# Six modulation vectors by one-column and broadcast matmuls, an opening without a stop, and a dense layer's last block by token tile

## Chip, cores and metric

One core of one Trainium2 chip runs the whole network. The metric is the device time of one execution in microseconds (us). The engines are TensorE (PE, matmuls), VectorE (DVE), ScalarE (ACT), GpSimd (POOL) and SyncE (SP, which issues the loads of weights).

## What is computed

Eight residual steps act on 256 tokens of width 1024. Each is conditioned on a vector c: a step's shift, scale and gate are slices of silu(c) @ w + b, and its input is h = norm(x) * (1 + scale) + shift. The layer inside a step is a mixer (steps 1 and 3), a dense SwiGLU of inner width 2816 (steps 2, 6 and 8), eight routed experts (step 4) or two kinds of attention (steps 5 and 7).

```python
def modulation(c, w, b):
    m = jnp.einsum("bd,de->be", jax.nn.silu(c), w) + b
    shift, scale, gate = jnp.split(m, 3, axis=-1)

def swiglu(h, w1, w3, w2):
    a = jnp.einsum("btd,df->btf", h, w1)
    g = jnp.einsum("btd,df->btf", h, w3)
    return jnp.einsum("btf,fd->btd", jax.nn.silu(a) * g, w2)

# steps 1 to 4 (layers 0 and 1): post-norm with a gain and a bias
x = layer_norm(DN_ALPHA * x + (1.0 + gate) * y, post_ln_g[layer, i], post_ln_b[layer, i])
# steps 5 to 8: h from rms_norm(x), and
x = x + g_a * (o @ w_out[l])
```

## The kernel before

The two token tiles of 128 (t = 0, 1) stay on chip throughout, and every weight is read once, in loads of 1 MB (`raw`, four buffers). A dense product is made of three passes (lines 178 to 180): ACT rounds the weight into a high part (line 159), DVE makes the low part by subtraction (line 160), and PE multiplies high by high, low by high and high by low. All engines run their own queues in order; a scheduler fixes the order of each queue when the program is built, from priorities. `behind()` keeps work that is issued early behind a step's residual, and `self.free` counts the weight splits that may pass this bar; before, that is the first split after step 1.

A modulation vector (layer, part, name) is written (l, s, SC), (l, s, SH) or (l, s, GA) for scale, shift and gate. Its 1024 x 1024 slice of w comes in four loads. `plan` says in which step a vector is made, for use one step later (a gate: at the end of the step after its scale's use begins); `fill(n)` spreads the loads over the step. There are two ways:

- `mod_rows` (line 301): DVE multiplies each row block of w by the entry of silu(c) that belongs to its partition and adds up, eight operations of 128 x 1024 (lines 318 and 320), into `macc`. `mod_done` then sums over partitions on PE: for a scale or shift eight matmuls with `macc` as the stationary operand and a column of ones (line 348), for a gate two matmuls of 512 columns with a matrix of ones.
- `mod_gate_pe` (line 281), for the gate (0, 0) alone: 16 matmuls of 512 columns multiply the raw weight by a broadcast entry of silu(c), in fp32, plus one per half for the bias row.

The opening (`run`): `setup` makes small constants; x is loaded and normalized; `fill(KD * KD)` makes (0,0,SC) and then (0,0,SH) by `mod_rows`, the column of the one being finished on PE and DVE ahead of the other's first product; then the rest of `setup` (`columns`, line 402: three transposes and copies) and `make_h` (line 511), which transposes x, applies scale and shift and splits the result for the projections.

The routing at step 4: `fill(KD * KD)` makes (2,0,SC), (2,0,SH) and (2,0,GA), all used in step 5, then `make_hf` transposes x, and `route` multiplies by the router, picks two experts a token and builds the lists that `experts` works through. `resid_rms` (line 591) ends the step with the gate (1,1).

A dense layer (`ffn`, line 673) runs over 11 blocks of 256 inner columns: project both halves, silu, multiply, and two blocks later `down` adds the block's part of the output to four accumulators (two token tiles by two halves). The last two blocks' `down` runs at the end, for t = 0 and then for t = 1:

```python
        for t in range(2):
            self.down(accs, [b for q in pend for b in block(*q)], t)
```

`resid` (line 549) follows, tile by tile: multiply by the gate (line 558), add x, statistics, and the normalized tile (line 586 or 588).

Of the kernel before, what the change touches and what calls it, by code (L numbers as in the profile page):

```python
# [19 lines left out]
D = 1024  # L20
# [47 lines left out]
class _Net:  # L68
# [82 lines left out]
    def split_now(self, v):  # L151

        k, n = v.shape[1], v.shape[2]
        H, L = [], []
        for z in range(0, k, k // 2):
            m = k // 2
            h = self.tl("hi", [128, 1024], F32R)[:, :m * n].rearrange("p (k n) -> p k n", k=m)
            l = self.tl("lo", [128, 1024], F32R)[:, :m * n].rearrange("p (k n) -> p k n", k=m)
# [23 lines left out]
    def mm(self, out, lhsT, rhs, start=True, stop=True):  # L182
        self.nc.tensor.matmul(out, lhsT=lhsT, rhs=rhs, start=start, stop=stop)  # L183
# [116 lines left out]
    def mod_rows(self, key):  # L300
# [13 lines left out]
        for i in range(2):  # L314
            k = self.modpos + i
            c = self.csil[:, c0 + k:c0 + k + 1]
            if k == 0 and not row:
                V.tensor_scalar(acc, v[:, i], c, None, ALU.mult)
            else:
                V.scalar_tensor_tensor(acc, v[:, i], c, acc, ALU.mult, ALU.add)  # L320

    def mod_done(self, key):

        if key in self.gates_pe:
# [11 lines left out]
        c = self.tl("col", [128, KD])  # L336
# [9 lines left out]
        else:  # L346
# [3 lines left out]
            sums = p[:, 0:KD]  # L350
        q = ((l * 2 + s) * 3 + j) * KD if l < 2 else ((l - 2) * 6 + j) * KD
# [4 lines left out]
    def mod(self, l, s, name):  # L356
        assert (l, s, name) in self.mods, (l, s, name)
        return self.mods[(l, s, name)]


    def setup(self):
# [19 lines left out]
        nc.gpsimd.memset(self.zero, 0.0)  # L381
        p = self.ps()
# [3 lines left out]
        self.off = {}  # L386

        def stack(tag, names, eng):

            r = self.sc([128, 128])  # L390
# [10 lines left out]
        def columns(tag, r, q):  # L401
            p = self.ps()
# [22 lines left out]
        self.identb = self.tl("const", [128, 128], BF16, tag="identb")
        V.tensor_copy(self.identb, self.ident)
        self.maskb = self.tl("const", [128, 384], BF16, tag="maskb")
        nc.gpsimd.memset(self.maskb, 0.0)
        V.tensor_copy(self.maskb[:, 0:128], cst[:, C_NEG:C_RT])
        V.tensor_copy(self.maskb[:, 256:384], cst[:, C_NEG:C_RT])  # L430
# [118 lines left out]
    def resid(self, get, x, gate, ln, norm=True):  # L549
# [39 lines left out]
        if norm:  # L589
            self.bar, self.free = self.last.ins, self.step == 1  # L590
# [85 lines left out]
    def ffn(self, h, w1, w3, w2, fill):  # L676
# [10 lines left out]
        for i in range(nstep):  # L687
            pss = []
            if i == 0:
# [15 lines left out]
            W2 = self.wrow(w2, 2 * i)  # L705
# [795 lines left out]
    def run(self):  # L1501
        a, nc = self.a, self.nc
        FFN = dict(f=2, s2=10, sh=12, pp=4, pa=4)
# [9 lines left out]
            0: [(0, 0, SC), (0, 0, SH)],  # L1513
# [3 lines left out]
            4: [(2, 0, SC), (2, 0, SH), (2, 0, GA)],  # L1517
# [4 lines left out]
        self.gates_pe = {(0, 0, GA)}  # L1522
# [3 lines left out]
        with self.phase(sh=12, s1=1, s2=3, pp=4, pa=4):  # L1526
            setup = self.setup()
            next(setup)
            self.mod_start(plan[0])
            x = self.load_x(a["x"])  # L1530
            xn = x = self.layer_norm(x)
            self.fill(KD * KD)
            for _ in setup:
                pass
            g, b = self.c1("ln0_g", 0), self.c1("ln0_b", 0)
            self.later = [lambda x=x: self.affine(x, a["ln0_g"], a["ln0_b"])]
        for s in range(1, 9):
# [5 lines left out]
            with self.phase(**SIZES[s]):  # L1543
# [4 lines left out]
                if s == 4:  # L1548
# [67 lines left out]
```

## Time and profile before

| what | value |
|---|---|
| device time, median of 3 runs | 2068.33 us (2067.39 to 2068.36) |
| the profiled execution: its own time / span of its trace | 2068.1 / 2066.0 us |
| busy: PE / DVE / ACT / POOL | 1926.2 / 1643.8 / 1208.2 / 50.2 us |
| bytes moved; mean rate | 555.25 MB; 269 GB/s |
| stretches: head, steps 1, 2, 3 | 0 to 45, to 175, to 377, to 513 us |
| routing, experts, step 5 | 513 to 564, to 1365, to 1524 us |
| steps 6, 7, 8 with the store | to 1726, to 1862, to 2066 us |

A stretch ends where PE's last matmul of the step does. Times in the trace count from the span's start. A matmul's duration includes its way through the array, so neighbours overlap, and what one costs is the distance between starts. A matmul in fp32 shows as two records, or, where the trace joins equal neighbours, as a row with their count (x16). The square bracket at a row's end is the time its engine was idle just before and the instruction that ended the wait. "PEclk" is the mean clock that TensorE was granted, as a share of 2.4 GHz; it has two levels, 1.00 and 0.50. Up to 50 us the profile shows 1.00 because nothing is recorded before the first change; there durations tell.

### The profile page before, as it was taken

Reading aid. Unit: us, or ns where it says so; the run is one execution under the profiler, and the core shown is the slowest. Engines: PE = TensorE matmul, PEld = TensorE weight load, DVE = VectorE, ACT = ScalarE, POOL = GpSimd, SP = SyncE. Lnnn points to the kernel's source line nnn. Section 1 sums busy time; section 2 is a strip of 40 time slices with the busy share of each in tenths; the row PEclk is TensorE's granted clock in tenths of the full one; section 3 lists DMA queues with packets and bytes.
Section 4 is the critical chain, followed back from the end, with each engine's and each line's share of the span. In section 5 each row is a group of like instructions: output and inputs, shape, how many; then the busy total and the mean of one; then the engine's idle time right before and its main releaser. Section 6 shows DMA issues by size and latency. Waiting matters only on the chain.

```text
span 2066.0 us, 29939 instructions
## 1 busy us (share of the span) xinstructions
PE 1926.2 (93%) x11481; PEld 1660.4 (80%) x11481; DVE 1643.8 (80%) x2412; ACT 1208.2 (58%) x1817; POOL 50.2 (2%) x100
## 2 busy tenths in 40 slices
PE   3998999898499999999999999969989999998999
PEld 3887999886378787878778888858869998978998
DVE  6888987898598888888888888889778887667554
ACT  3455445562488767767776777755554546555442
POOL 4000000100000000000000000000000000000000
PEclk9999999998699999999999999979999999999999
DMA  9576999665399999899999999958339995326662
GB/s 325 184 276 214 348 329 316 195 223 205 144 330 362 339 332 341 319 357 346 345 326 350 348 355 358 364 187 279 138 119 349 335 328 164 123 86 220 204 204 82
DMA packets 283238, 555.25 MB, mean 269 GB/s; under 512 B 10172, under 2 KB 137520, under 8 KB 283088
## 3 DMA queue, kind: packets, MB, share of 16 engines
q1 hardware_dynamic: 280000, 549.49, 75.1%
q0 software_dynamic: 2656, 3.20, 0.9%
q8 instruction: 91, 1.49, 0.3%
q10 hardware_dynamic: 432, 0.58, 0.1%
q14 instruction: 59, 0.48, 0.1%
HBM read 552.19 MB, written 1.05 MB: 268 GB/s over the span
## 4 chain that ended last, share of the span: by engine, by line
PE 63%; DVE 6%; ACT 2%; issue 2%; DMA 0%; ACTq 0%; DVEq 0%
PE pp L179 11%; PE pp L180 11%; PE pp L178 11%; PE pa L654 6%; PE ya L179 4%; PE ya L178 4%; PE ya L180 4%; PE pp L187 3%; DVE lo L160 2%; PE pj L178 2%; PE pj L179 1%; PE pj L180 1%; PE sa L183 1%; PE pp L183 1%; ACT hi L159 1%
## 5 line engine op out<-in xcount | busy, mean ns | idle before, releaser
L160 DVE TENSOR_TENSOR lo<-raw,hi 128x1024 fp32r<-128x1024 f32 x660 | 786.0, 1219 | 177.3 <-ACT hi L159 168.6
L159 ACT CAST hi<-raw 128x1024 fp32r<-128x1024 f32 x660 | 667.4, 1050 | 344.2 <-PE pp L179 141.8
L178 PE MATMUL pp<-h,hi 128*128 128x256 f32 x960 | 270.7, 282 | 0.0
L180 PE MATMUL pp<-h,lo 128*128 128x256 f32 x960 | 267.8, 279 | 0.0
L179 PE MATMUL pp<-h,hi 128*128 128x256 f32 x960 | 267.7, 279 | 0.0
L160 DVE TENSOR_TENSOR lo<-rawx,hi 128x1024 fp32r<-128x1024 f32 x176 | 208.3, 1219 | 40.2 <-ACT hi L159 38.9
L320 DVE SCALAR_TENSOR_TENSOR macc<-raw,const,macc 128x1024 f32<-128x1024 f32 x168 | 215.2, 1281 | 9.9 <-DMA raw<-in_w_mod_dram 7.1
L180 PEld LDWEIGHTS pp<-h,lo 128*128 128x128 f32 x960 | 182.2, 190 | 0.1
L159 ACT CAST hi<-rawx 128x1024 fp32r<-128x1024 f32 x176 | 176.9, 1050 | 9.2 <-PE pp L180 7.4
L179 PEld LDWEIGHTS pp<-h,hi 128*128 128x128 f32 x960 | 180.6, 188 | 1.7 <-issue 1.2
L178 PEld LDWEIGHTS pp<-h,hi 128*128 128x128 f32 x960 | 180.3, 188 | 1.7 <-ACT hi L159 1.0
L179 PE MATMUL pp<-lo,h 128*128 128x512 f32 (+1 forms) x480 | 174.9, 365 | 1.3 <-DVE lo L160 1.0
L178 PE MATMUL pj<-hi,h 128*128 128x256 f32 x576 | 168.3, 293 | 7.2 <-ACT h L530 4.0
L178 PE MATMUL pp<-hi,h 128*128 128x512 f32 (+1 forms) x480 | 173.5, 362 | 0.2 <-ACT f L528 0.2
L179 PE MATMUL pj<-lo,h 128*128 128x256 f32 x576 | 165.1, 288 | 1.8 <-DVE lo L160 1.8
L180 PE MATMUL pj<-hi,h 128*128 128x256 f32 x576 | 164.8, 288 | 0.0
L654 PE MATMUL pa<-hi,s 128*128 128x512 f32 x528 | 148.2, 390 | 0.0
L179 PE MATMUL pp<-lo,xe 128*128 128x512 f32 (+1 forms) x384 | 144.9, 377 | 1.2 <-DVE lo L160 1.0
L180 PE MATMUL pp<-hi,x 128*128 128x512 f32 (+1 forms) x384 | 143.7, 374 | 0.0
L178 PE MATMUL pp<-hi,xe 128*128 128x512 f32 (+1 forms) x384 | 143.6, 374 | 0.0
L180 PE MATMUL pp<-hi,xe 128*128 128x512 f32 (+1 forms) x384 | 143.1, 373 | 0.0
L179 PE MATMUL ya<-lo,s 128*128 128x512 f32 x352 | 140.8, 400 | 0.0
(474 smaller groups left out, 3518.5 us busy)
## 6 DMA issues: line engine op xcount, KB each, us to landing
raw<-in_moe_w_dram SPq DMA_DIRECT2D x176, 1024.0 KB, 6.3
rawx<-in_moe_w_dram SPq DMA_DIRECT2D x88, 1024.0 KB, 6.3
raw<-in_ada_w_dram SPq DMA_DIRECT2D x48, 1024.0 KB, 6.7
raw<-in_w_mod_dram SPq DMA_DIRECT2D x48, 1024.0 KB, 6.9
raw<-in_w_in_dram SPq DMA_DIRECT2D x42, 1024.0 KB, 6.0
raw<-in_ffn_w_dram SPq DMA_DIRECT2D x33, 1024.0 KB, 6.3
raw<-in_w_gate_dram SPq DMA_DIRECT2D x22, 1024.0 KB, 5.2
raw<-in_w_up_dram SPq DMA_DIRECT2D x22, 1024.0 KB, 5.3
```

Of the source, the lines that this page charges most:

```text
L159: self.nc.scalar.copy(h, v[:, z:z + m])
L160: self.nc.vector.tensor_tensor(l, v[:, z:z + m], h.bitcast(F32), ALU.subtract)
L178: mm(out, lhsT=a[0], rhs=b[0], start=start, stop=False)
L179: mm(out, lhsT=a[0], rhs=b[1], start=False, stop=False)
L180: mm(out, lhsT=a[1], rhs=b[0], start=False, stop=stop)
L183: self.nc.tensor.matmul(out, lhsT=lhsT, rhs=rhs, start=start, stop=stop)
L187: self.nc.tensor.transpose(out, in_, self.ident[:p, :p])
L320: V.scalar_tensor_tensor(acc, v[:, i], c, acc, ALU.mult, ALU.add)
L654: mm(accs[t][h], lhsT=y[ia][:, s], rhs=W[ib][:, h * 512:(h + 1) * 512], start=start and ia == 0 and ib == 0, stop=stop and ia == 1)
```

## The change

Five things change. (1) `mod_first` opens the program: the shift's first product goes to ACT, DVE runs through both vectors' products, the columns are finished after both, and 20 bf16 matmuls of zeros (`warm`) stand on PE between the scale's and the shift's column matmuls; `setup` yields twice more, so that one of its copies is made early and two after `make_h`. (2) `mod_cols_pe` makes (0,1,SH), (2,0,SC), (2,0,SH) and (2,1,SH): per load 16 matmuls of one column with the raw weight as the stationary operand and an entry of silu(c) as the moving one, and a small DVE addition. (3) The gates (1,1) and (2,0) go through `mod_gate_pe`; (2,0,GA) moves from the routing to behind the experts. (4) `ffn` works its last block by token tile, in the natural layout (tokens on partitions), with four transposes more, and W2 of the block before has pools of its own (`wh`, `wl`). (5) Two splits may pass the bar after steps 2 and 6.

```diff
@@ def fill
                 if key in self.gates_pe:
                     self.mod_gate_pe(key)
+                elif key in self.cols_pe:
+                    self.mod_cols_pe(key)
@@
+    def mod_cols_pe(self, key):
...
+        v = self.raw(wv[:, self.modpos:self.modpos + 2, j * D:(j + 1) * D])
+        p = self.ps(pool=self.mps)
+        for q in range(KD):
+            for i in range(2):
+                k = c0 + self.modpos + i
+                self.mm(p[:, q:q + 1], v[:, i, q * 128:(q + 1) * 128], self.csil[:, k:k + 1], i == 0, i == 1)
+        if self.modpos == 0:
+            V.scalar_tensor_tensor(self.modacc, p[:, 0:KD], 1.0 if key[2] == "scale" else 0.0, self.mod_bias(key), ALU.add, ALU.add)
+        else:
+            V.tensor_tensor(self.modacc, self.modacc, p[:, 0:KD], ALU.add)
@@ def mod_rows
-            if k == 0 and not row:
+            if k == 0 and act:
+                nc.scalar.activation(acc, v[:, i], ACT.Copy, scale=c)
+            elif k == 0 and not row:
@@
+    def warm(self, p, n, after):
+
+        with self.tc.issue_after(after):
+            for _ in range(n):
+                self.nc.tensor.matmul(p.rearrange("p (q n) -> p q n", n=128), lhsT=self.zero[:, 0:128], rhs=self.zero[:, None, :].to_broadcast([128, 4, 128]), start=True, stop=True)
+
+    def mod_first(self, scale, shift, setup):
+
+        V = self.nc.vector
+        ps = []
+        for key in (scale, shift):
+            for k in range(0, KD, 2):
+                self.modpos = k
+                self.mod_rows(key, key == shift)
+            p = self.ps()
+            for k in range(KD):
+                self.mm(p[:, k:k + 1], self.modacc[:, k * 128:(k + 1) * 128], self.ones[:, 0:1])
+            ps.append(p)
+            if key == scale:
+                next(setup)
+                self.warm(self.ps(), 20, self.pe_last.ins)
+        with self.tc.issue_after(self.mod_last.ins):
+            next(setup)
+            for key, p in zip((scale, shift), ps):
+                self.mods[key] = self.mod_col(key, p[:, 0:KD])
@@ def resid
-            self.bar, self.free = self.last.ins, self.step == 1
+            self.bar, self.free = self.last.ins, {1: 1, 2: 2, 6: 2}.get(self.step, 0)
@@ def ffn
-        for t in range(2):
-            self.down(accs, [b for q in pend for b in block(*q)], t)
+
+        Ws = [self.wcol(w, i * 256) for w in (w1, w3)]
...
+        for t in range(2):
+            s = slice(t * 128, (t + 1) * 128)
+            for p, W in zip(pss, Ws):
+                for k in range(KD):
+                    self.mm3(p[:, t], (h[0][:, k, s], h[1][:, k, s]), (W[0][k], W[1][k]), k == 0, k == KD - 1)
+            S.activation(sa[:, t], pss[0][:, t], ACT.Silu)
+            V.tensor_tensor(gn[:, t], sa[:, t], pss[1][:, t], ALU.mult)
+            for q in pend:
+                self.down(accs, block(*q), t)
+            for j in range(2):
+                self.tr(gp[:, j, s], gn[:, t, j * 128:(j + 1) * 128])
...
+            self.down(accs, block((gh, gl), W2, i), t)
@@ def run
-            4: [(2, 0, SC), (2, 0, SH), (2, 0, GA)],
+            4: [(2, 0, SC), (2, 0, SH)],
...
-        self.gates_pe = {(0, 0, GA)}
+        self.gates_pe = {(0, 0, GA), (1, 1, GA), (2, 0, GA)}
+        self.gps = "pa"
+        self.cols_pe = {(0, 1, SH), (2, 0, SC), (2, 0, SH), (2, 1, SH)}
...
-            self.fill(KD * KD)
-            for _ in setup:
-                pass
+            self.mod_first((0, 0, SC), (0, 0, SH), setup)
...
                     get = lambda t, hh: ysum[t][hh]
+
+                    self.gps = "pp"
+                    self.mod_start([(2, 0, GA)])
+                    self.fill(KD)
+                    self.gps = "pa"
```

PE's queue before, at step 4's routing, from the last matmul of step 3 to the router's matmuls (`macc` 5419 and 5447 are the scale and the shift (2,0), 5475 is the gate (2,0), `x` the normalized tokens, `sh` the router):

```order
L654 MATMUL pa_5189<-hi_5274,h_4720 128x512
L183 MATMUL pp_5437<-const_115,macc_5419 128x1 x8
L183 MATMUL pp_5465<-const_115,macc_5447 128x1 x8
...
L183 MATMUL pp_5495<-macc_5475,const_115 128x512
L183 MATMUL pp_5498<-macc_5475,const_115 128x512
L187 MATMUL pp_5502<-const_113,x_5327 128x128 x4
...
L187 MATMUL pp_5523<-const_113,x_5327 128x128 x4
L183 MATMUL pp_5532<-sh_5530,h_5501 128x8 x16
```

Here the transposes stand behind 16 column matmuls and the gate's two.

The same place of PE's queue now (`raw` are loads of the scale and the shift (2,0), `const_127` is silu(c)):

```order
L719 MATMUL pa_5283<-hi_5368,h_4814 128x512
L182 MATMUL pp_5516<-const_127,raw_5514 128x1 x16
L182 MATMUL pp_5536<-const_127,raw_5534 128x1 x16
...
L182 MATMUL pp_5637<-const_127,raw_5635 128x1 x16
L182 MATMUL pp_5657<-const_127,raw_5655 128x1
L186 MATMUL pp_5676<-const_113,x_5421 128x128 x4
L182 MATMUL pp_5657<-const_127,raw_5655 128x1 x15
...
L186 MATMUL pp_5697<-const_113,x_5421 128x128 x4
L182 MATMUL pp_5706<-sh_5704,h_5675 128x8 x16
```

There are now 128 column matmuls in eight groups, seven groups and one matmul of them ahead of the first transpose, and the gate is gone.

PE's queue now in step 1, toward the end of the mixer (`raw` are loads of the shift (0,1), `pj` is a projection, L715 begins the output projection):

```order
L177 MATMUL pj_1516<-hi_1512,h_348 128x256
L182 MATMUL pa_1420<-const_127,raw_1418 128x1
L178 MATMUL pj_1516<-lo_1513,h_348 128x256
L182 MATMUL pa_1420<-const_127,raw_1418 128x1
L179 MATMUL pj_1516<-hi_1512,h_349 128x256
L182 MATMUL pa_1420<-const_127,raw_1418 128x1 x5
L182 MATMUL pa_1577<-const_127,raw_1575 128x1 x16
L182 MATMUL pa_1597<-const_127,raw_1595 128x1 x16
L715 MATMUL pj_1653<-raw_1657,ml_1101 128x512
```

Two of the four groups alternate with a projection's matmuls, and two stand back to back; before, DVE did this sum and eight column matmuls followed.

PE's queue now behind the experts (`ya` is their sum, `pa` the residual's input, `raw` 16898 to 16919 the gate (2,0)'s loads, `x` the normalized tokens of step 5):

```order
L179 MATMUL ya_16036<-hi_16859,s_16828 128x512
L182 MATMUL pp_16896<-raw_16898,const_127 128x512
L182 MATMUL pa_5754<-s_16875,s_14869 128x512
...
L182 MATMUL pp_16896<-raw_16898,const_127 128x512 x3
L182 MATMUL pp_16896<-raw_16904,const_127 128x512 x4
L182 MATMUL pp_16911<-gate_16894,const_115 128x512
L182 MATMUL pp_16911<-raw_16913,const_127 128x512 x4
L182 MATMUL pp_16911<-raw_16919,const_127 128x512 x4
...
L186 MATMUL pp_17035<-const_113,x_16930 128x128 x4
```

The gate's 16 matmuls came in between the residual's input and the transposes for step 5; on SP's queue its four loads stand ahead of `post_ln_g`, `post_ln_b` and step 5's first weights.

## Rows read from the trace of the kernel before

**Rows 1.** The page: busy us (share of the span) and instructions of each engine.

```profile
PE 1926.2 (93%) x11481; PEld 1660.4 (80%) x11481; DVE 1643.8 (80%) x2412; ACT 1208.2 (58%) x1817; POOL 50.2 (2%) x100
```

**Rows 2.** Busy time by stretch (start:end, length, busy us of PE, PEld, DVE, ACT, POOL, PEclk, DMA).

```profile
50.00:175.00 125.00, 124.56 (x792) 101.78 (x792) 102.12 (x217) 58.67 (x123) 2.93 (x8) 1.00 0.64 222
384.00:490.00 106.00, 95.39 (x662) 85.35 (x661) 94.71 (x198) 56.00 (x126) 3.05 (x10) 0.90 0.62 213
1400.00:1450.00 50.00, 46.21 (x377) 43.50 (x376) 46.04 (x92) 26.56 (x47) 0.00 (x0) 1.00 0.87 299
```

**Rows 3.** Step 1, PE: gate matmuls as a group, then the timeline (start, us, engine).

```profile
L183 PE MATMUL pa<-raw,const 128*128 128x512 f32 x32 | 15.1, 601 | 0.0
...
169.42 0.39 PE L654 MATMUL pa<-hi,h 128*128 128x512 f32 x1
169.65 0.28 PE L183 MATMUL pa<-const,macc 128*128 128x1 f32 x2
169.79 0.47 PE L654 MATMUL pa<-hi,h 128*128 128x512 f32 x1
170.24 0.47 PE L654 MATMUL pa<-lo,h 128*128 128x512 f32 x1
```

**Rows 4.** Timeline of the head, DVE and then PE.

```profile
26.08 0.17 DVE L353 SCALAR_TENSOR_TENSOR col<-pp,const 128x8 f32<-128x8 f32 x1 [3.73 <-PE pp L183]
26.94 9.21 DVE L320 SCALAR_TENSOR_TENSOR macc<-raw,const,macc 128x1024 f32<-128x1024 f32 x7
...
36.21 3.57 PE L183 MATMUL pp<-const,macc 128*128 128x1 f32 x16 [10.17 <-DVE macc L320]
45.02 0.57 PE L178 MATMUL pj<-hi,h 128*128 128x256 f32 x1
```

**Rows 5.** Timeline at the ends of steps 2, 6, 4, and in step 5.

```profile
371.57 1.29 DVE L558 TENSOR_TENSOR x<-pa,gate 128x512 f32<-128x512 f32 x2 [3.05 <-PE pa L654]
379.44 0.82 DVE L586 TENSOR_SCALAR x<-x,t,t 128x1024 f32<-128x1024 f32 x1
383.62 0.81 DVE L586 TENSOR_SCALAR x<-x,t,t 128x1024 f32<-128x1024 f32 x1
...
380.41 1.07 PE L187 MATMUL pa<-const,x 128*128 128x128 f32 x8 [3.21 <-DVE x L586]
383.49 0.80 PE L178 MATMUL pj<-hi,h 128*128 128x256 f32 x2 [2.01 <-ACT h L530]
...
1727.75 1.06 PE L187 MATMUL pp<-const,x 128*128 128x128 f32 x8 [1.01 <-DVE x L588]
...
1383.73 1.12 PE L187 MATMUL pp<-const,x 128*128 128x128 f32 x4 [12.37 <-DVE x L615]
...
1415.59 0.38 PE L178 MATMUL pj<-hi,h 128*128 128x256 f32 x1 [1.50 <-DVE qk L1391]
```

**Rows 6.** Timeline of PE from step 3's last matmul to the router.

```profile
512.82 3.62 PE L183 MATMUL pp<-const,macc 128*128 128x1 f32 x32
516.31 1.02 PE L183 MATMUL pa<-const 128*128 128x512 bf16 x4
531.72 3.55 PE L183 MATMUL pp<-macc,const 128*128 128x512 f32 x4 [14.39 <-DVE macc L320]
539.70 5.15 PE L183 MATMUL pp<-sh,h 128*128 128x8 f32 x32 [0.78 <-DVE h L508]
```

**Rows 7.** PEclk by stretch, columns as in rows 2.

```profile
516.30:517.80 1.50, 1.03 (x6) 0.30 (x5) 1.39 (x8) 0.00 (x0) 0.19 (x1) 1.00 0.02 3
517.80:531.50 13.70, 0.00 (x0) 0.00 (x0) 13.63 (x15) 7.45 (x7) 0.00 (x0) 0.50 0.64 230
535.10:541.70 6.60, 4.38 (x35) 3.62 (x33) 4.10 (x6) 2.64 (x5) 0.00 (x0) 1.00 1.04 392
541.80:558.80 17.00, 9.07 (x41) 8.64 (x40) 3.57 (x21) 1.81 (x3) 0.00 (x0) 0.50 0.14 55
1367.80:1391.60 23.80, 8.56 (x35) 6.96 (x35) 21.99 (x61) 11.88 (x26) 0.00 (x0) 0.50 0.31 98
```

More of the change, by code (lines that the diff above doesn't have):

```diff
@@ L149, in split, with split_now @@
             return self.split_now(v)
-    def split_now(self, v):
+    def split_now(self, v, pools=("hi", "lo")):
         k, n = v.shape[1], v.shape[2]
@@ L156, in split_now @@
             m = k // 2
-            h = self.tl("hi", [128, 1024], F32R)[:, :m * n].rearrange("p (k n) -> p k n", k=m)
-            l = self.tl("lo", [128, 1024], F32R)[:, :m * n].rearrange("p (k n) -> p k n", k=m)
+            h, l = (self.tl(p, [128, 1024], F32R)[:, :m * n].rearrange("p (k n) -> p k n", k=m) for p in pools)
             self.nc.scalar.copy(h, v[:, z:z + m])
@@ L182, in mm @@
     def mm(self, out, lhsT, rhs, start=True, stop=True):
-        self.nc.tensor.matmul(out, lhsT=lhsT, rhs=rhs, start=start, stop=stop)
+        self.pe_last = self.nc.tensor.matmul(out, lhsT=lhsT, rhs=rhs, start=start, stop=stop)
     def tr(self, out, in_):
@@ L350, in mod_done, with mod_col @@
             sums = p[:, 0:KD]
+        return self.mod_col(key, sums)
+    def mod_col(self, key, sums):
+        l, s, name = key
+        j = self.mod_src(key)[2]
+        c = self.tl("col", [128, KD])
         q = ((l * 2 + s) * 3 + j) * KD if l < 2 else ((l - 2) * 6 + j) * KD
@@ L358, in mod @@
         return self.mods[(l, s, name)]
+    def warm(self, p, n, after):
[3 more added lines that the diff above has]
+    def mod_first(self, scale, shift, setup):
+        V = self.nc.vector
+        ps = []
[14 more added lines that the diff above has]
+                self.mods[key] = self.mod_col(key, p[:, 0:KD])
     def setup(self):
@@ L381, in setup @@
         nc.gpsimd.memset(self.zero, 0.0)
+        self.identb = self.tl("const", [128, 128], BF16, tag="identb")
+        V.tensor_copy(self.identb, self.ident)
+        self.maskb = self.tl("const", [128, 384], BF16, tag="maskb")
+        nc.gpsimd.memset(self.maskb, 0.0)
+        V.tensor_copy(self.maskb[:, 0:128], cst[:, C_NEG:C_RT])
+        V.tensor_copy(self.maskb[:, 256:384], cst[:, C_NEG:C_RT])
         p = self.ps()
@@ L385, in setup @@
         S.activation(self.csil, p[:, 0:16], ACT.Silu)
-        self.off = {}
+        self.off, self.off2 = {}, []
+        vecs = self.tl("lo", [128, 1024])
         def stack(tag, names, eng):
-            r = self.sc([128, 128])
+            r = vecs[:, len(self.off2) * 128:(len(self.off2) + 1) * 128]
+            self.off2.append(tag)
             q = 0
@@ L401, in columns @@
         def columns(tag, r, q):
-            p = self.ps()
+            p = self.ps(pool="pp" if "pp" in self.pools else "sd")
             self.tr(p[:, 0:q], r[:q])
@@ L421, in setup @@
         yield
-        self.col1 = columns("col1", *r1)
+        p1 = self.ps()
+        self.tr(p1[:, 0:r1[1]], r1[0][:r1[1]])
+        yield
+        self.col1 = self.tl("const", [128, r1[1]], tag="col1")
+        V.tensor_copy(self.col1, p1[:, 0:r1[1]])
+        yield
         self.col2 = columns("col2", r2, q)
         self.col4 = columns("col4", *r4)
[L425 to L430, printed above, removed]
         o = self.off
@@ L688, in ffn @@
             pss = []
+            if i == nstep - 1:
+                break
             if i == 0:
@@ L704, in ffn @@
                     pss.append(p)
-            W2 = self.wrow(w2, 2 * i)
+            if i == nstep - 2:
+                W2 = self.split_now(self.raw(w2.rearrange("(k p) n -> p k n", p=128)[:, 2 * i:2 * i + 2, :]), ("wh", "wl"))
+            else:
+                W2 = self.wrow(w2, 2 * i)
             sa = self.sc([128, 2, T])
@@ L723, in ffn @@
             self.fill(fill[i % len(fill)])
-        for t in range(2):
-            self.down(accs, [b for q in pend for b in block(*q)], t)
+        Ws = [self.wcol(w, i * 256) for w in (w1, w3)]
+        W2 = self.wrow(w2, 2 * i)
+        pss = [self.ps((128, 2, T)) for _ in range(2)]
+        sa, gn = self.sc([128, 2, T]), self.sc([128, 2, T])
+        gp = self.ps((128, 2, T))
+        gh, gl = self.sc([128, 2, T], F32R), self.sc([128, 2, T], F32R)
+        for t in range(2):
+            s = slice(t * 128, (t + 1) * 128)
[8 more added lines that the diff above has]
+                self.tr(gp[:, j, s], gn[:, t, j * 128:(j + 1) * 128])
+            S.copy(gh[:, :, s], gp[:, :, s])
+            V.tensor_tensor(gl[:, :, s], gp[:, :, s], gh[:, :, s].bitcast(F32), ALU.subtract)
+            self.down(accs, block((gh, gl), W2, i), t)
         return lambda t, hh: accs[t][hh]
@@ L1562, in run @@
                     get = lambda t, hh: ysum[t][hh]
+                    self.gps = "pp"
+                    self.mod_start([(2, 0, GA)])
+                    self.fill(KD)
+                    self.gps = "pa"
                 else:
                     h = self.make_h(xn, A, B)
+                    with self.tc.high_priority(offset=-40):
+                        for _ in setup:
+                            pass
                     self.mod_start(plan.get(s, []), LAG.get(s, 0))
```

23 lines of the change are left out of this document (15 added, 8 removed).

## The prediction, made before the changed kernel ran

> **What bounds the kernel now.** I read the page first. The matrix engine (PE) is busy for 1926 us, 93% of the span [rows 1], so most of the span is simply its matmuls, and an instruction added to PE is paid in full unless it falls where PE waits. The timeline, stretch by stretch, then shows where PE waits, and the granted clock (PEclk, 1.00 for 2.4 GHz and 0.50 for 1.2 GHz) shows where its work takes twice as long. Steps 1 and 5, where two of the six moved vectors go, are stretches in which PE hardly waits: 124.56 of 125 us busy and 46.21 of 50 [rows 2]. The places where PE does wait are the head, the ends of steps, the softmax of step 3, and the routing.
>
> **The price of a moved vector.** In the old form a scale or shift cost DVE eight row products (9.21 us for seven of them [rows 4], so near 10) and PE eight one-column matmuls, two records each: 3.62 us for the 32 records of two vectors at full clock [rows 6], so 1.8 us a vector and 0.226 us a matmul. At the low clock the same eight take 3.57 us [rows 4], 0.446 each. In the new form the stationary operand is the raw weight, of the same type and size, and a vector takes 64 such matmuls: 64 x 0.226 = 14.5 us, at the low clock 28.5. Does such a matmul hide between wide ones? The timeline of step 1 answers: with 512-column matmuls back to back, starts are 0.23 us apart (169.42, and the next instruction at 169.65); with a column matmul after each they are 0.45 apart (169.79 to 170.24) [rows 3]. The difference, 0.22, is the whole price. So the move costs PE 14.5 - 1.8 = 12.7 us a vector.
>
> **Head: -6.** Today the shift's products start only when the scale's column is finished: DVE waits 3.73 us, makes the first product from 26.08 to 26.94 and the other seven in 9.21 us, and PE adds 3.57 us of column matmuls after that; the first projection starts at 45.02 [rows 4]. In the change ACT makes the first product and DVE runs straight on: 3.73 + 0.8 = 4.5 us. The 20 zero matmuls run while DVE sums; if they bring the clock up the shift's columns take 1.8 instead of 3.57, another 1.8. Together 6.3; I take 6. Bounds: 2 (loads late, clock stays low) and 9 (the first projections, a record of 0.57 us at 45.02 [rows 4] against one of 0.38 at full clock [rows 5], speed up as well).
>
> **Step 1: +15.** The vector (0,1,shift) costs the 12.7 us above on a PE that has no free time. The last two of its four groups stand back to back, 32 column matmuls or 7.2 us; what that does to the clock is argued at the routing, and I add 2.5 for it. Bounds 9 (DVE, which gives up 10 us and is busy 82% here [rows 2], returns a little) and 20.
>
> **Ends of steps 2, 6 and 8: -4, -2.5, 0.** Today tile 0's sums are ready 5.5 us before tile 1's, and DVE is still in tile 0's normalization when PE is done: tile 0's normalized x is made at 379.44, tile 1's at 383.62, and PE waits 3.21 us for the first and 2.01 for the first operand of the projections [rows 5]. With the last block by token tile, tile 1 still has its 24 matmuls of 512 columns (0.23 us each [rows 3], 5.5 us) and 48 of half that width (as long) to go when tile 0 is done: 11 us, enough for tile 0's whole chain (371.57 to 380.2, 8.6 us [rows 5]). What is late next is tile 1's own chain, which then starts unhindered: about 4.5 us from PE's last matmul (two pairs of 0.6 us, statistics, the root's small operations, 0.8) instead of 7.2. I take 4 of the 5.2 at step 2, bounds 1 and 7; 2.5 at step 6, where PE waits 1.01 us for tile 0 [rows 5] and again for tile 1, bounds 0 and 4; nothing at step 8, where only the store follows and tile 1 ends when it did. Each end adds four transposes, 0.13 us each (1.07 for eight [rows 5]): +1.2 in all is kept for them, with bounds 0 and 3 for waits on the new copies.
>
> **Step 3: -3.** The gate (1,1) moves to PE: 16 matmuls of 512 columns, the 32 records of 0.6 us that take 15.1 us in step 1 [rows 3], less some 2 us for its old two: +13. It meets a stretch with room: from 384 to 490 PE is idle for 10.6 of 106 us, and the granted clock is 0.90 on the mean [rows 2], so that a fifth, 21 us, ran at 1.2 GHz; the waits lie there, and I estimate PE's work in it at 11 us, which would take 5.5 less at 2.4. The order shows projections and gate matmuls between the softmax's steps, and DVE, busy 94.71 us of the stretch [rows 2], loses two vectors' products. If all is filled, 13 - 10.6 - 5.5 = -3. Bounds -8 and +8.
>
> **Routing: +31.** Today two vectors' columns run at 512.82, PE waits 14.39 us for DVE's sum of the gate (2,0), and the router's matmuls start at 539.70, 26.9 us after 512.82 [rows 6]. The change takes the gate away, but puts 128 column matmuls ahead of the transposes on a queue that keeps its order. Nothing here needs those two vectors (they are for step 5), yet the router, the token lists and the first experts all wait behind them. At full clock: 128 x 0.226 = 28.9, zeros 0.9, the transposes left 1.7, DVE's copies 0.8: 32.3, or 5.4 later. Will the clock hold? At 516.31 PE went from 3.6 us of one-column matmuls to 1 us of zeros, and the clock was already at 0.50 from 517.8 on, after half a microsecond of waiting [rows 6, 7]; it was up again for the gate's transposes and fell during the router's 32 records of 8 columns, which had no wait among them (1.00 to 541.7, 0.50 from 541.8) [rows 7]. Both times narrow matmuls stood before the fall. The Trainium skill, TensorE: Matmul & The Clock Gate, Part 1 (What's actually happening), says the clock falls back after the engine has been idle; an engine that issues without a break is not, and by that rule the term would be 5.4, not 31. The row decides, for me: some 5 us at full clock (today 512.82 to 517.8 [rows 6, 7]; 22 matmuls), 106 x 0.446 = 47.3 after that, zeros 1.8, transposes 3, copies 0.8, so 57.9, and the router starts 31 later. Bounds 3 and 36. The eight loads are no limit: four fit in the buffers, and the next four, 1 MB each, have over 10 us each.
>
> **End of the experts: -3.** The gate (2,0) now runs on PE behind the experts: 16 matmuls, 15.1 us, while DVE makes the residual with another gate and PE waits, 12.37 us of it in one piece [rows 5]. It keeps the clock up: from 1367.8 to 1391.6 that is 0.50 today, and of the 8.56 busy us there [rows 7] some 7.3 are not zeros and would take half, -3.6. Against it: four loads of 1 MB go ahead of the normalization's rows and of step 5's first weights on SP's queue, and those wait for buffers that the gate's matmuls release. I take +1 for that, bounds -6 and +9.
>
> **Step 5: +11.** 12.7 for (2,1,shift), less the 3.8 us that PE waits in 1400 to 1450, where DVE is busy 92% [rows 2], plus 2 for the clock at two adjoining groups. Bounds 5 and 17.
>
> **Sum.** -6 + 15 - 4 - 2.5 + 1.2 - 3 + 31 - 3 + 11 = +39.7, on the profiled execution's own 2068.1 us (2066.0 of span and 2.1 around it; the median of the runs is 2068.33, the same within 0.02%). That is **2108 us**. A change of 0.2%, 4 us, is about what can be told from none.
>
> **Rivals.** (a) *The column matmuls hold the clock*: routing +5.4, steps 1 and 5 +12.7 and +8.9, so 39.7 - 25.6 - 2.3 - 2.1 = +9.7: **2078**. For it: there was a wait, if a short one, before each of the two falls. Against: a wait of 1.50 us before 1415.59 [rows 5] brought no fall, the clock is 1.00 from 1400 to 1450 [rows 2]. It is the outcome that the section of the Trainium skill cited above would give. (b) *The same, and the cold stretches of today go too*: the route's 9.07 busy us at 541.8 to 558.8 [rows 7] halve (-4.5), the head gains 3 more, step 2's end 2: **2068**, no change. (c) *DVE, not PE, sets the pace of steps 1 and 5*. Then a vector's 10 us on DVE come back and its column matmuls run in PE's slack: steps 1 and 5 give -10 each in place of +15 and +11, so 39.7 - 46 = -6: **2062**, faster, though the routing costs its 31. It decides where PE's idle time exceeds the 12.7 us that it is given; for it DVE's 92% [rows 2], against it PE's 0.4 us of idle in step 1 [rows 2]. (d) *Step 5 starts late*: the normalization's rows land after DVE needs them and the first weights after the transposes, +9 at the experts' end in place of -3: **2120**. (e) That the zero matmuls don't keep the clock until the shift's columns come would cost 4 us of the head's 6; it lies inside the forecast's own range, 2093 to 2122.
>
> **Chances.** Forecast 0.46, (a) 0.18, (b) 0.14, (c) 0.12, (d) 0.10. Of (b) a part falls on either side of 0.2%: 0.08 faster, 0.05 same, 0.01 slower; of (a) 0.02 is within 0.2%. So faster 0.20, same 0.07, slower 0.73. The range leaves out (c), the fast part of (b), and the top of (d): 2064 to 2122; the forecast's own is 2093 to 2122.
>
> **What would show it.** Routing: 256 one-column records between step 3's last matmul and the router; a mean of 0.22 us and PEclk 0.50 for most of it proves the forecast, 0.113 rival (a). Steps 1 and 5: records of one column between 256-column ones, starts 0.34 apart, DVE below 80%. Head: no DVE wait between the two runs of products, first projection near 39. Step 2's end: PE's two waits under 2 us together. Experts' end: PEclk 1.00 up to the projections. The forecast is wrong if the router starts less than 40 us after step 3's last matmul, or if step 1 lasts no longer than it does.

## The result: 2165 us, and the profile after

The changed kernel takes 2165.19 us (median of 4 runs, 2160.39 to 2169.08) against 2068.35 us: a ratio of 1.0463, 95% interval 1.0447 to 1.0478. It is slower by 97 us, where 40 were forecast; the direction was right, and the size lay above the range.

The page of the changed kernel first: its span, and busy time by engine, which answers to [rows 1].

```profile
span 2164.6 us, 31007 instructions
PE 2069.0 (96%) x12025; PEld 1779.5 (82%) x12025; DVE 1596.9 (74%) x2381; ACT 1211.9 (56%) x1826; POOL 48.7 (2%) x98
```

PE is busy for 143 us more (2069.0 against 1926.2) in a span that is 98.6 us longer; DVE gave up 47 us. The stages say where. Each is the time between two starts on PE in the traces: the first matmul of a projection, of the router or of an expert, and the last matmul into the output accumulators; the last two columns belong to the experiments below.

| stage, us | before | changed | no columns (e1) | 64 wide (e4) |
|---|---|---|---|---|
| to the first projection | 45.0 | 42.6 | 44.5 | 44.5 |
| step 1 to its last matmul | 130.1 | 160.2 | 133.2 | 143.5 |
| to step 2's projections | 10.2 | 10.6 | 10.2 | 11.5 |
| step 2 to its last matmul | 191.5 | 193.2 | 193.7 | 193.9 |
| to step 3's projections | 6.7 | 4.3 | 4.3 | 4.3 |
| step 3 to its last matmul | 129.1 | 129.3 | 136.3 | 128.1 |
| to the router | 27.1 | 57.9 | 22.3 | 33.1 |
| to the first expert | 24.8 | 32.6 | 26.6 | 29.2 |
| experts | 798.2 | 801.8 | 801.0 | 799.5 |
| to step 5's projections | 24.7 | 24.8 | 25.2 | 25.2 |
| step 5 to step 6's projections | 146.4 | 171.1 | 146.7 | 162.3 |
| steps 6, 7, 8 and the store | 532.3 | 536.4 | 534.4 | 534.7 |
| span | 2066.0 | 2164.6 | 2078.4 | 2109.8 |

Three rows carry 85.5 of the 98.6 us: step 1 (+30.1), the way to the router (+30.8) and step 5 (+24.7). Busy time and clock by stretch, with the columns of [rows 2], show what they have in common:

```profile
147.40:181.50 34.10, 34.10 (x144) 30.89 (x144) 6.51 (x25) 3.13 (x7) 0.00 (x0) 0.50 0.35 123
543.30:598.00 54.70, 54.06 (x251) 52.52 (x250) 8.44 (x26) 5.54 (x6) 0.00 (x0) 0.50 0.45 148
598.00:630.50 32.50, 19.35 (x87) 18.31 (x87) 13.55 (x33) 14.62 (x23) 0.00 (x0) 0.50 0.32 109
1529.80:1543.40 13.60, 13.60 (x65) 13.60 (x65) 0.47 (x4) 2.02 (x6) 0.00 (x0) 0.50 0.39 121
1567.30:1581.00 13.70, 13.70 (x57) 12.13 (x57) 4.02 (x18) 3.78 (x13) 0.00 (x0) 0.50 0.39 137
```

In every one the granted clock is 0.50, and in step 1 (147.4 to 181.5) and step 5 (the last two) PE is busy for the whole of it, 34.10 of 34.10 us in step 1. Before, step 1 stood at 1.00 from 50 us to its end [rows 2]. The timeline of PE in step 1 shows the fall itself:

```profile
146.47 0.36 PE L177 MATMUL pj<-hi,h 128*128 128x256 f32 x1
146.67 0.28 PE L182 MATMUL pa<-const,raw 128*128 128x1 f32 x2
146.81 0.36 PE L178 MATMUL pj<-lo,h 128*128 128x256 f32 x1
...
147.61 0.56 PE L177 MATMUL pj<-hi,h 128*128 128x256 f32 x1
147.97 0.42 PE L182 MATMUL pa<-const,raw 128*128 128x1 f32 x2
148.25 0.56 PE L178 MATMUL pj<-lo,h 128*128 128x256 f32 x1
```

A 256-column matmul and a one-column matmul take turns without a break. A pair's distance is 0.34 us at first (146.47 to 146.81), as priced, and from 147.4 on 0.64 (147.61 to 148.25). The routing, in the timeline of PE, answers to [rows 6]:

```profile
540.32 10.92 PE L182 MATMUL pp<-const,raw 128*128 128x1 f32 x64
552.76 34.56 PE L182 MATMUL pp<-const,raw 128*128 128x1 f32 x162
588.07 6.40 PE L182 MATMUL pp<-const,raw 128*128 128x1 f32 x30
597.98 6.94 PE L182 MATMUL pp<-sh,h 128*128 128x8 f32 x32
610.10 2.28 PE L182 MATMUL pp<-t,const 128*128 128x8 f32 x10 [5.18 <-DVE t L1175]
619.38 0.55 PE L182 MATMUL pp<-s,x 128*128 128x256 f32 x1 [7.00 <-DVE s L1241]
630.53 0.78 PE L177 MATMUL pp<-hi,xe 128*128 128x512 f32 x1
```

The 64 + 162 + 30 records are the 128 column matmuls. The first 64 still begin at full clock; 162 records in 34.56 us are 0.213 each. The router starts 57.9 us after step 3's last matmul (540.09). Behind it PE waits longer than before for DVE (5.18 us now, 2.06 before), because DVE makes the first experts' low parts between the small operations of the route. PE's row of the kernel before, and DVE's timeline now:

```profile
546.91 2.27 PE L183 MATMUL pp<-t,const 128*128 128x8 f32 x10 [2.06 <-DVE t L1086]
...
605.38 0.28 DVE L1165 TENSOR_TENSOR sh<-t 128x128 f32<-128x128 f32 x1
605.58 1.22 DVE L159 TENSOR_TENSOR lo<-raw,hi 128x1024 fp32r<-128x1024 f32 x1
606.72 0.28 DVE L1167 TENSOR_TENSOR sh<-sh,const 128x128 f32<-128x128 f32 x1
606.92 1.22 DVE L159 TENSOR_TENSOR lo<-raw,hi 128x1024 fp32r<-128x1024 f32 x1
```

### The profile page after: what moved, and what is told of

Its sections match the earlier page's. It is cut to its first block, busy times and chain, and to the rows that moved or that the text cites. A ratio compares the mean times of both kernels' runs of the same rounds, so it can differ in the third digit from the quotient of the medians.

```text
span 2164.6 us, 31007 instructions
## 1 busy us (share of the span) xinstructions
PE 2069.0 (96%) x12025; PEld 1779.5 (82%) x12025; DVE 1596.9 (74%) x2381; ACT 1211.9 (56%) x1826; POOL 48.7 (2%) x98
## 4 chain that ended last, share of the span: by engine, by line
PE 61%; DVE 6%; ACT 3%; issue 2%; DMA 1%; DVEq 0%; ACTq 0%
PE pp L178 11%; PE pp L179 10%; PE pp L177 10%; PE pa L719 6%; PE ya L178 4%; PE ya L177 3%; PE ya L179 3%; DVE lo L159 2%; PE pp L186 2%; PE pp L182 2%; PE pj L177 1%; PE pj L178 1%; PE pj L179 1%; PE sa L182 1%; ACT hi L158 1%
## 5 line engine op out<-in xcount | busy, mean ns | idle before, releaser
L177 PE MATMUL pp<-h,hi 128*128 128x256 f32 x864 | 243.7, 282 | 0.0
L178 PE MATMUL pp<-h,hi 128*128 128x256 f32 x864 | 240.9, 279 | 0.0
L179 PE MATMUL pp<-h,lo 128*128 128x256 f32 x864 | 240.9, 279 | 0.0
L178 PE MATMUL pp<-lo,h 128*128 128x512 f32 (+1 forms) x576 | 201.9, 351 | 1.3 <-DVE lo L159 1.0
L177 PE MATMUL pp<-hi,h 128*128 128x512 f32 (+1 forms) x576 | 200.7, 349 | 0.2 <-ACT f L593 0.2
L158 ACT CAST hi<-rawx 128x1024 fp32r<-128x1024 f32 x176 | 176.9, 1050 | 11.5 <-PE pp L179 9.6
L177 PE MATMUL pj<-hi,h 128*128 128x256 f32 x576 | 173.1, 301 | 6.9 <-ACT h L595 4.9
L179 PE MATMUL pj<-hi,h 128*128 128x256 f32 x576 | 170.0, 297 | 0.0
L347 DVE SCALAR_TENSOR_TENSOR macc<-raw,const,macc 128x1024 f32<-128x1024 f32 x124 | 159.0, 1283 | 13.1 <-DMA raw<-in_ada_w_dram 6.8
L179 PEld LDWEIGHTS pp<-h,lo 128*128 128x128 f32 x864 | 164.0, 190 | 0.0
L178 PEld LDWEIGHTS pp<-h,hi 128*128 128x128 f32 x864 | 162.5, 188 | 1.7 <-issue 1.2
L177 PEld LDWEIGHTS pp<-h,hi 128*128 128x128 f32 x864 | 162.2, 188 | 1.7 <-issue 0.7
L179 PE MATMUL ya<-hi,s 128*128 128x512 f32 x352 | 137.7, 391 | 0.0
```

The lines of the kernel that those rows point to most:

```text
L177: mm(out, lhsT=a[0], rhs=b[0], start=start, stop=False)
L178: mm(out, lhsT=a[0], rhs=b[1], start=False, stop=False)
L179: mm(out, lhsT=a[1], rhs=b[0], start=False, stop=stop)
L347: self.mod_last = V.scalar_tensor_tensor(acc, v[:, i], c, acc, ALU.mult, ALU.add)
```

## Experiments: the columns, the clock, and each part alone

**The vectors back on DVE, all or in part.** Only the set of vectors differs from the changed kernel:

```diff
@@ e1_no_cols
-        self.cols_pe = {(0, 1, SH), (2, 0, SC), (2, 0, SH), (2, 1, SH)}
+        self.cols_pe = set()
@@ e2_route_back
-        self.cols_pe = {(0, 1, SH), (2, 0, SC), (2, 0, SH), (2, 1, SH)}
+        self.cols_pe = {(0, 1, SH), (2, 1, SH)}
@@ e3_steps_back
-        self.cols_pe = {(0, 1, SH), (2, 0, SC), (2, 0, SH), (2, 1, SH)}
+        self.cols_pe = {(2, 0, SC), (2, 0, SH)}
```

> The changed kernel with the four vectors of cols_pe made by DVE again; the opening, the gates and the last block by token tile stay changed. Theory C (the one-column matmuls carry the whole loss: 12.7 us of PE each plus the low clock that follows them): step 1 gives back about 30 us, step 5 about 24, the way from step 3's last matmul to the first expert 30 to 39, so 2065 to 2085 us. Theory R (the last block by token tile, the gates or the opening also cost): it stays above 2090.

> Only (2,0,scale) and (2,0,shift) go back to DVE, so the routing has no 128 column matmuls on PE's queue. Theory C: 30 to 39 us less than the changed kernel, 2125 to 2135, with steps 1 and 5 as slow as there. Rival: the routing then waits for DVE's two sums as it once waited for the gate's, and less than 20 us come back, 2145 or more.

> Only (0,1,shift) and (2,1,shift) go back to DVE, in steps 1 and 5. Theory C: step 1 shorter by 25 to 30 us and step 5 by 20 to 24, no stretch at 1.2 GHz inside them, 2105 to 2120. Rival (PE's load alone counts, 12.7 us a vector): 25 us less in all, 2140.

Measured, one run each: e1 2080.22 us, e2 2128.95, e3 2111.30. So the four vectors cost 85 us of the 97, the routing's two 36 and those of steps 1 and 5 54. The two parts together come to 90, more than both at once; 4.4 of the 5 us lie in step 3, which takes 136.3 us in e1, 134.5 in e2 and 126.7 in e3 (129.3 in the changed kernel). With the sums of (2,0) on DVE, PE waits for DVE there, in the timeline of e1:

```profile
507.77 2.07 PE L186 MATMUL sd<-const,ys 128*128 128x128 f32 x8 [4.62 <-DVE ys L1101]
```

Ahead of `ys` DVE works through six products of those sums, of 0.75 to 1.28 us, among its small operations (499.98 to 507.36). The changed kernel and e3 have no such wait. Theory C holds for each total. In its details e3 misses: short stretches at 1.2 GHz are left inside its steps 1 and 5 (146.3 to 149.7 us is one), where none was expected. The other 12 us (e1 against before) belong to the other parts.

**The same matmuls, 64 columns wide.** Is it the matmuls' number and place, or that so little passes through the array? The moving operand is repeated 64 times, and DVE reads the first of each 64 results:

```diff
-                self.mm(p[:, q:q + 1], v[:, i, q * 128:(q + 1) * 128], self.csil[:, k:k + 1], i == 0, i == 1)
+                self.mm(p[:, q * 64:(q + 1) * 64], v[:, i, q * 128:(q + 1) * 128], self.csil[:, k:k + 1].to_broadcast([128, 64]), i == 0, i == 1)
```

> The same matmuls in the same number, but with 64 equal columns in the moving operand in place of one; DVE adds the first of each 64. Theory C (the clock falls because so few columns pass): the stretches at 1.2 GHz in step 1, the routing and step 5 shrink or go, the way to the router takes about 34 us in place of 58, and the total falls by 40 to 65 us, to 2100 to 2125. Rival Q (number and place of the matmuls alone): no gain, or some us slower for the wider operand, 2160 to 2175.

It takes 2111.62 us, 54 less than the changed kernel, by wider instructions in the same number. By stretch (step 1's columns, the routing to the router, the rest of the routing) and in the timeline of PE:

```profile
145.00:180.00 35.00, 35.00 (x225) 29.45 (x225) 16.03 (x36) 11.76 (x20) 0.00 (x0) 1.00 0.49 176
525.90:558.80 32.90, 31.54 (x278) 30.85 (x276) 11.58 (x34) 6.69 (x8) 0.53 (x1) 1.00 0.70 233
558.80:588.00 29.20, 15.50 (x85) 14.62 (x86) 11.89 (x31) 13.32 (x21) 0.00 (x0) 0.59 0.41 137
...
526.01 6.58 PE L182 MATMUL pp<-const,raw 128*128 128x64 f32 x58
533.79 18.20 PE L182 MATMUL pp<-const,raw 128*128 128x64 f32 x162
558.83 1.39 PE L182 MATMUL pp<-sh,h 128*128 128x8 f32 x11 [1.10 <-DVE h L573]
```

The clock is 1.00 through both places. 162 records take 18.20 us, 0.112 each: what the one-column ones cost at full clock [rows 6], so the 64 columns are free. The table's last column gives the clock's share by subtraction: 160.2 - 143.5 = 16.7 us in step 1, 24.8 on the way to the router, 3.4 behind it, 8.7 in step 5. What is left of the vectors in steps 1 and 5 is the price of issue, forecast at 12.7 each. Over the kernel before it is 13.3 and 15.9 us; over e1, which has the same opening and the vectors on DVE, 10.2 and 15.7. In e4's step 5 the clock still fell once (1521.0 to 1527.8). Rival Q falls.

**Each other part alone, on the kernel before.** p1 takes over `mod_first`, `warm`, `mod_col` and the changed `setup`, with the lines for them in `mod_rows` and `run`; p2 the changed `ffn` and `split_now`, the pools `wh` and `wl`, and the new `self.free`, all as in the diff of the change. p3 and p4 each move one gate:

```diff
@@ p3_gate11
-        self.gates_pe = {(0, 0, GA)}
+        self.gates_pe = {(0, 0, GA), (1, 1, GA)}
@@ p4_gate20
-            self.modps = self.ps(pool="pa")
+            self.modps = self.ps(pool=self.gps)
...
-            4: [(2, 0, SC), (2, 0, SH), (2, 0, GA)],
+            4: [(2, 0, SC), (2, 0, SH)],
...
-        self.gates_pe = {(0, 0, GA)}
+        self.gates_pe = {(0, 0, GA), (2, 0, GA)}
+        self.gps = "pa"
...
+                    self.gps = "pp"
+                    self.mod_start([(2, 0, GA)])
+                    self.fill(KD)
+                    self.gps = "pa"
```

> The kernel before with the new opening alone. Theory C says that the opening is not where the loss is: first projection 1 to 2.5 us earlier, and up to 3 us lost in step 1, where two copies and a transpose now lie and the clock starts low again: 2066 to 2071 us. Theory R (the opening is worth the 6 us that were forecast): 2060 to 2063.

> The kernel before with the last block of the dense layers by token tile and the changed rule for splits, alone. From the stages of the changed kernel: 2.4 us gained between step 2's last matmul and step 3's projections, 2 us lost in each of steps 2 and 6 and none or 2 in step 8: 2068 to 2071 us. The forecast's terms (-4, -2.5, +1.2) would give 2063.

> The kernel before with the gate (1,1) alone made on PE from the raw weight. If it fills PE's waits in step 3 as the changed kernel's step 3 suggests (129.3 us against 129.1, with 13 us more of work), 2064 to 2070 us and no stretch at 1.2 GHz between 466 and 487; if DVE still holds the softmax up, step 3 grows by 7 to 13 us, 2075 to 2081.

> The kernel before with the gate (2,0) alone taken from the routing to PE behind the experts. Forecast's mechanism: the router starts 5 to 12 us sooner after step 3's last matmul, and 2 to 3 us come from the clock before step 5; against it the routing stays at 1.2 GHz throughout, since the gate's wide matmuls no longer raise the clock, +3, and the bias row's matmul, +1.4: 2058 to 2066 us. Rival (the wait only changes its name, to DVE's sums of scale and shift): 2067 to 2072.

One run each, against 2069.25 us of the kernel before on that chip: p1 2069.69, p2 2066.65, p3 2078.12, p4 2071.24. Only p3 is clear of the runs' spread (the kernel before ran from 2062.8 to 2072.1 in all); for the others the stages are the evidence. p1: 0.9 us sooner at the first projection, lost again in step 1. p2: 2.4 us gained at step 2's end, about 2 lost inside step 2, and 4.4 gained in step 3, which none of the theories had. There PE waits 3.3 us for DVE's `P`, the softmax's result, in place of 6.7; what lets DVE be earlier is open. p3's total lies in the second alternative: its step 3 takes 134.2 us, 5 more (7 to 13 were expected), and the way to the first expert 5 more. DVE still makes the sums of (2,0) there, and PE waits for it as in e1 (4.64 us at `ys`). So the gate's matmuls were free only where those sums went too, as in the changed kernel. p4: the router starts 5.5 us sooner (21.6 against 27.1), as expected, and 3.1 of it are lost before the first expert, 3.7 in the experts. Its total is in the rival's range, but not for the rival's reason: the columns of scale and shift run at 514.12, straight behind step 3, without a wait. The routing of p4 is at 0.55 on the mean:

```profile
513.90:563.30 49.40, 29.02 (x139) 25.48 (x138) 20.73 (x60) 15.12 (x24) 0.52 (x1) 0.55 0.19 65
```

The gate's two wide matmuls had raised the clock for the router [rows 7]; without them it stays low from 516.5 to 560.8, 2.5 us before the first expert.

**Zeros in the waits.** If the clock beside a wait is what costs, matmuls that compute nothing should pay. w1 is p2 with this in `make_h`, w2 has p4's move as well and zeros among the routing's matmuls:

```diff
+                n = {2: (15, 16), 3: (2, 8), 5: (50, 0), 6: (18, 5), 7: (4, 8), 8: (18, 5)}.get(self.step, (0, 0))[t]
+                if q == 0 and n:
+                    with self.tc.issue_after(self.pe_last.ins):
+                        for _ in range(n):
+                            nc = self.nc
+                            nc.tensor.matmul(p, lhsT=self.zero[:, 0:128], rhs=self.zero[:, None, :].to_broadcast([128, 4, 128]), start=True, stop=True)
                 for j in range(4):
                     k = q + j
                     self.tr(p[:, j], xn[:, t, k * 128:(k + 1) * 128])
```

> The kernel before with the last block by token tile (as p2_ffn_end), and with bf16 matmuls of zeros on PE ahead of the transposes of steps 2, 3, 5, 6, 7 and 8, as many as the waits there hold (15 and 16, 2 and 8, 50, 18 and 5, 4 and 8, 18 and 5 for the two tiles). No vector is moved. Theory C (where PE waits, what is lost is the clock as well): the stretches at 1.2 GHz at the steps' ends go, 2 to 4 us each at five places and 3.6 before step 5: 2050 to 2058 us. Rival (PE's waits set the time, the clock beside them costs nothing): 2066 to 2070, or more where the zeros outlast a wait.

> As w1_zeros, and the gate (2,0) on PE behind the experts in place of the 50 zeros there, with zeros in the routing's waits (32 of 256 columns among the transposes, 4 and 14 of 512 after the router). Theory C: the router starts 5 to 6 us sooner as in p4_gate20 and the routing keeps or regains 2.4 GHz, another 3 to 6 us, less 1.4 for the bias row: 4 to 9 us below w1_zeros. Rival (the zeros lengthen the routing's chain): level with w1_zeros or above.

w1 takes 2062.69 us (median of 8), a ratio of 0.9975 to the kernel before, interval 0.9962 to 0.9989; w2 2061.96 (median of 10), 0.9971, 0.9959 to 0.9984. Both beat both kernels, by less than was expected, and their intervals overlap. In w1, by stretch, around the starts of steps 2, 5, 6 and 8:

```profile
174.00:190.00 16.00, 15.51 (x101) 10.96 (x100) 15.14 (x31) 12.16 (x24) 0.07 (x1) 1.00 0.40 130
1362.00:1392.00 30.00, 21.72 (x128) 15.89 (x126) 25.48 (x67) 15.28 (x30) 0.00 (x0) 0.83 0.42 141
1522.00:1540.00 18.00, 15.02 (x118) 13.52 (x116) 16.63 (x21) 13.00 (x26) 0.56 (x1) 1.00 0.75 239
1858.00:1876.00 18.00, 16.46 (x124) 14.09 (x122) 16.63 (x28) 11.93 (x23) 0.00 (x0) 1.00 0.59 184
```

The clock is 1.00 but for step 5's start, where the zeros run out before the normalized tokens come. The same windows of the kernel before stood at 0.79, 0.60, 0.72 and 0.73:

```profile
174.00:190.00 16.00, 8.91 (x57) 8.12 (x56) 15.14 (x33) 12.59 (x25) 0.00 (x0) 0.79 0.30 105
1362.00:1392.00 30.00, 12.22 (x51) 9.31 (x50) 26.68 (x67) 17.48 (x32) 0.00 (x0) 0.60 0.37 118
1522.00:1540.00 18.00, 12.46 (x61) 10.98 (x60) 17.47 (x36) 13.36 (x31) 0.00 (x0) 0.72 0.35 115
1858.00:1876.00 18.00, 12.67 (x55) 10.51 (x54) 15.62 (x35) 10.90 (x25) 0.00 (x0) 0.73 0.37 123
```

2 to 4 us were expected at five places and 3.6 before step 5. Against p2, which has the same last block, the trace of w1 gains 1.5 us on the way to step 2's projections (9.1 us, where p2 has 10.6 and the kernel before 10.2) and 1.3 to 1.5 inside each of steps 3, 5, 7 and 8. The projections of steps 5, 6 and 8 begin no sooner, step 6 gains nothing, and those of steps 3 and 7 begin 0.4 and 0.7 us later. Stages with the same code differ by up to 1.4 us from one single trace to the next, so how much of the 6.5 us the zeros bring, and how much is p2's part (2.6 us in one run), is not separated. Step 3, 5.9 us shorter than in the kernel before, has 4.4 of that in p2 already. w2 misses its 4 to 9 us below w1: its router starts 5.1 us sooner than w1's, and its step 5 takes 5.1 us longer, for a reason that was not looked for. Why a faster clock shortens a step's start by so little (ACT and DVE prepare PE's first operands there) was not tried further.

## Why the prediction was right in sign and wrong in size

In the traces the kernel grew by 98.6 us, and the sum had 39.7. Of the 59 us that are missing, steps 1 and 5 hold 29, the ends of steps 2, 6 and 8 and the way from the router to the first expert 8 each, and the head, step 3, the experts and the experts' end 3 to 4 each. Rivals (a) to (c) need a clock that holds or a PE with slack, and the 57.9 us to the router and step 1's +30.1 are against them; (d) put step 5's start some 9 us later, and it came 0.1 later.

- **Price of issue: right by the records.** 12.7 us a vector was forecast. At full clock a one-column matmul takes two records of 0.112 us (e4), so 64 of them less the old 1.8 are 12.5. By the stages of e4 against e1 it was 10.2 us in step 1 and 15.7, one fall of the clock included, in step 5.
- **Routing to the router: right.** 57.9 us from step 3's last matmul were forecast, 57.9 measured, with the clock falling as argued from [rows 7]. That the two agree to a tenth is luck: the clock held for 3 us where 5 were taken, and a matmul at low clock took 0.43 us where 0.446 was. The section of the Trainium skill that was weighed there (TensorE: Matmul & The Clock Gate, Part 1, What's actually happening) ties the low clock to an idle engine. Here it came with an engine busy, by its records, for 34.10 of 34.10 us; the measurement decides.
- **Steps 1 and 5: the steps that failed.** "I add 2.5 for it" and "plus 2 for the clock at two adjoining groups" gave the low clock to the two groups that stand back to back. In step 1 it came earlier, while one-column matmuls still took turns with 256-column ones, and lasted 34 us. In step 5 it came where groups follow each other closely, but twice, for 13.6 and 13.7 us, and slowed the wide matmuls between and behind them too. The terms should have been 16.7 and 8.7, or more, in place of 2.5 and 2: 21 us. The reason given at the routing, that narrow matmuls stood before each fall, had not been carried over to narrow ones mixed with wide ones. The rest of step 1's 30.1 is the issue, 10.2, and 3.1 that e1's step 1 has too, from the opening (see the head). Of the 3.8 us of PE's waits that step 5 was to get back, there is no sign in e4's 15.7 against 12.7.
- **Router to first expert: left out of the sum.** +7.8 us. p4 and e4 give its parts. One is the low clock: p4, with the routing at low clock, loses 3.1, and the changed kernel takes 3.4 more than e4, whose clock held up to the router. The other part is DVE's splits of the first experts' weights, which now fall among the route's small operations: PE's wait there grew by 3.1 us, and e4 has it too.
- **Head: -2.4 in this trace, some -0.9 over all runs, not -6.** DVE runs straight on into the loads. In the timeline of DVE and of PE, and of PE in e1:

```profile
25.29 2.60 DVE L347 SCALAR_TENSOR_TENSOR macc<-raw,const,macc 128x1024 f32<-128x1024 f32 x2 [1.73 <-DMA raw<-in_ada_w_dram]
29.56 2.61 DVE L347 SCALAR_TENSOR_TENSOR macc<-raw,const,macc 128x1024 f32<-128x1024 f32 x2 [1.67 <-DMA raw<-in_ada_w_dram]
33.90 2.60 DVE L347 SCALAR_TENSOR_TENSOR macc<-raw,const,macc 128x1024 f32<-128x1024 f32 x2 [1.73 <-DMA raw<-in_ada_w_dram]
...
25.67 7.27 PE L396 MATMUL pp<-const 128*128 128x512 bf16 x20
36.56 2.17 PE L182 MATMUL pp<-const,macc 128*128 128x1 f32 x16 [3.62 <-DVE macc L347]
42.58 0.56 PE L177 MATMUL pj<-hi,h 128*128 128x256 f32 x1
...
37.07 3.58 PE L182 MATMUL pp<-const,macc 128*128 128x1 f32 x16 [5.31 <-DVE macc L347]
```

  Three waits for the shift's loads, 5.1 us together, take the place of the one that was removed: the bound "loads late" of that term. The zeros did their part in this trace, the column matmuls at 36.56 took 2.17 us instead of 3.57 [rows 4], and the clock fell again before the projections (0.56 us at 42.58). That was luck: in the five other runs with this opening PE waited 4.1 to 5.3 us for DVE behind the zeros, and the same matmuls took 3.1 to 3.6 us. So it went as rival (e) has it. The first projection came at 42.6 to 44.5 us in these six runs, at 44.3 to 45.0 in the six with the old opening. Behind it step 1 is longer, by 1.3 us in p1 and 3.1 in e1, where it runs at low clock until 56.1 us; in the kernel before the clock is up from 50.2 us on:

```profile
44.50:56.10 11.60, 11.60 (x41) 8.70 (x40) 9.45 (x12) 8.55 (x15) 0.78 (x1) 0.50 0.57 170
```

  No term had this.
- **Ends of steps 2, 6 and 8: not -5.3 with the transposes but +3.** The wait that was named shrank (0.79 us for tile 0 in place of 3.21 [rows 5], and the projections start 2.4 us sooner). The 2.01 us stayed: they are for tile 0's operand as well, which ACT makes behind tile 0's own transposes, so an earlier tile 0 moves them and does not shorten them. At step 6's end nothing was gained (5.3 us to step 7's projections, 5.2 before), and the last block by tile costs about 1.8 us within each of steps 2 and 6 and 2 in step 8 with the store. Here are PE's waits at step 2's end, in the timeline:

```profile
403.92 0.50 PE L719 MATMUL pa<-hi,s 128*128 128x512 f32 x1 [0.46 <-ACT s L812]
407.72 1.09 PE L186 MATMUL pa<-const,x 128*128 128x128 f32 x8 [0.79 <-DVE x L623]
410.83 0.58 PE L177 MATMUL pj<-hi,h 128*128 128x256 f32 x1 [2.01 <-ACT h L595]
```

- **Step 3: +0.2, not -3.** It took in the gate's 13 us almost whole, with the help of the 4.4 us that p2's part brings here. Most of the idle time of [rows 2] lay between 460 and 490 us; here are that window before and the same one, counted from step 3's projections, now:

```profile
460.00:490.00 30.00, 20.91 (x91) 15.99 (x90) 22.56 (x65) 12.77 (x38) 0.90 (x1) 0.72 0.47 165
...
487.30:517.30 30.00, 29.09 (x188) 23.48 (x187) 16.27 (x39) 14.72 (x29) 0.90 (x1) 1.00 0.52 176
```

- **Experts' end: 0, not -3; experts: +3.6.** The gate's matmuls kept the clock up to 1454, but PE then waited 3.75 us for DVE's work on the tokens and the clock fell at the transposes after all:

```profile
1435.35 6.17 PE L182 MATMUL pp<-raw,const 128*128 128x512 f32 x14
1442.50 7.13 PE L182 MATMUL pp<-raw,const 128*128 128x512 f32 x16
1454.03 1.36 PE L186 MATMUL pp<-const,x 128*128 128x128 f32 x8 [3.75 <-DVE sh L1447]
1457.17 0.58 PE L177 MATMUL pj<-hi,h 128*128 128x256 f32 x1
```

  So DVE, not PE's clock, sets this stretch: it took 24.8 us with the clock up to 1454, 24.7 before with it at 0.50 for most of it [rows 7]. The forecast's -3.6 took PE's work there for what step 5 waits for. The experts begin at low clock (2.3 us, by lining up their matmuls with those of the kernel before) and end with one matmul for the bias row among theirs (1.3 us by the same).

## What to carry to other kernels

A sum over a matrix's rows can go to PE only if PE has the time: here it costs 14.5 us of PE to spare DVE 10. Price every new matmul at both clocks, and look for narrow ones among them, mixed with wide ones too; where narrow ones must be issued, a wider moving operand may cost nothing. And before a removed wait is booked, look whether the loads behind it come in time.

## What was not expected of the hardware

The granted clock fell to 1.2 GHz while PE issued without a break, even where one-column and 256-column matmuls took turns (147.4 us), and it stayed there for 34 us. The same matmuls with 64 equal columns took the same 0.112 us a record and kept 2.4 GHz. Wide matmuls of zeros, which compute nothing, kept the clock at 1.00 through waits where it had been 0.72 to 0.79, and gained little by it: the projections of steps 6 and 8 began no sooner.
